# A two-layer encoder in fp32: order of the little products in gate and up, turns between VectorE and GpSimd, and new places

## The chip, the cores and the metric

The kernel runs on one core of a Trainium2 chip. The metric is the device time of one launch in microseconds; lower is better. Three runs of the kernel before took 604.31, 604.35 and 604.79 us, so its median is 604.35 us. TensorE, the matrix engine, is called PE here; DVE is VectorE, ACT is ScalarE, POOL is GpSimd, and SP only issues transfers.

## The reference

Two encoder layers on 256 positions of 1024 features, all in fp32. The mixer projects to three groups of heads (neighbourhood, dilated, grouped-query attention), normalises and rotates, attends, and projects back. The channel sublayer is where most of the time goes:

```python
def channel_sublayer(x, n2, w_gu, cw, cb, w_dn):
    h = rms_norm(x, n2)
    g, u = jnp.split(h @ w_gu, 2, axis=-1)
    g = depthwise_conv_centred(g, cw, cb)
    return x + (jax.nn.gelu(g, approximate=False) * u) @ w_dn

for l in range(DEPTH):                      # DEPTH = 2, S = 256, D_FF = 2816
    x = mixer_sublayer(x, norm1_g[l], w_in[l], q_norm_g[l], k_norm_g[l], rpb[l],
                       out_norm_g[l], w_out[l], tables)
    x = channel_sublayer(x, norm2_g[l], w_gate_up[l], conv_w[l], conv_b[l], w_down[l])
```

## The kernel before

**Products.** An fp32 product is made of three products of split operands: each operand is a rounded high part (hi) and the rest (lo), and hi·hi, hi·lo and lo·hi are summed in PSUM. Weights arrive by DMA as `wp_raw`; for each unit of weights (`unit`, `split`, lines 683 to 715) ScalarE casts raw to `wp_hi` and VectorE subtracts to get `wp_lo`. The layer's input, scaled and transposed by PE and ScalarE, is `act_hT`, whose lo half is made by VectorE (`split_T`, line 731).

**The feed-forward part.** The 2816 features go in 11 steps of two blocks (j = 0, 1) of 128 features. A step has a gate (G), an up (U) and a down (D); the list `FFN` (line 77) gives their order. Gate and up run `half_up` (line 1346) on one unit of weights. For each block there are eight *large* products (a 128x128 piece of the weight's hi against 512 columns, which are hi and lo of the input side by side) and eight *little* ones (a piece of the weight's lo against the 256 columns of the input's hi). All sixteen of a block sum into one PSUM bank, `ps[j]`, a buffer of the pool `psw`. In the rows, large is `psw_w<-act_hT,wp_hi ... 128x512` and little is `psw_w<-act_hT,wp_lo ... 128x256`. The order is large 0, little 0, large 1, little 1, eight each; the first gate of a layer has an order of its own. Down adds 24 matmuls of 512 columns into four banks `psa_a`. In the last step of the last layer the last of its four column pieces is halved, into 256 columns in `psa` and 256 in a bank of `psw` (`end`), so that the output can go out in pieces.

**The order of the work.** Nothing is issued where it is written. Every operation is recorded in a `Plan` (class at line 239), with a cost from `cost` (line 475), and so all instructions show one line in the profile, L472. `Plan.order` (line 323) is a list scheduler: it keeps, for each engine, the time at which it comes free, takes among all ready operations the one that can start first, and among equals the one of the lowest rank. The rank is the operation's number in the program plus a shift for some kinds of work plus an entry of the table `PLACES` (line 229), which moves single operations by hand:

```python
o.rank = i + self.shift + PLACES.get(i, 0)
...
if at is not None and (best is None or (at, o.rank, i) < best):
    best = (at, o.rank, i)
...
else:
    free[e], end = at + o.ns, at + o.lat
```

The order that comes out is fixed at build time. On the chip each engine runs its list in that order, and waits where an operand or a buffer is late.

**The start and the tail.** Before the first projections ScalarE casts the first weights, scales the eight transposes of the input into `act_hT` and squares the input for its norm (`mean_squares`, line 755; `act_s2k<-const_x`). At the end VectorE adds the sums to `const_x` piece by piece (the lines behind `down(last)`, about 1476), and SP sends each piece out.

## Time and profile before

| | |
|---|---|
| median of three runs | 604.35 us |
| the profiled execution's own time | 604.39 us |
| its span in the trace | 602.6 us |
| PE busy | 596.9 us, 3496 matmuls |
| DVE busy | 484.9 us |
| ACT busy | 428.5 us |
| POOL busy | 81.0 us |
| TensorE clock granted | full in every slice |

The busy time of an engine says how much work it has; only the chain that ended last, and the gaps in an engine's timeline, say what bounds the end. A row of a timeline groups neighbouring instructions of one kind: the start of the first, then the time from there to the end of the last, which overlaps the next row since matmuls are pipelined. So the pace of PE is read from start to start.

### The profile page before, as it was taken

Reading aid. Unit: us, or ns where it says so; the run is one execution under the profiler, and the core shown is the slowest. Engines: PE = TensorE matmul, PEld = TensorE weight load, DVE = VectorE, ACT = ScalarE, POOL = GpSimd, SP = SyncE. Lnnn points to the kernel's source line nnn. Section 1 sums busy time; section 2 is a strip of 40 time slices with the busy share of each in tenths; the row PEclk is TensorE's granted clock in tenths of the full one; section 3 lists DMA queues with packets and bytes.
Section 4 is the critical chain, followed back from the end, with each engine's and each line's share of the span. In section 5 each row is a group of like instructions: output and inputs, shape, how many; then the busy total and the mean of one; then the engine's idle time right before and its main releaser. Section 6 shows DMA issues by size and latency. Waiting matters only on the chain.

```text
span 602.6 us, 9916 instructions
## 1 busy us (share of the span) xinstructions
PE 596.9 (99%) x3496; PEld 524.7 (87%) x3496; DVE 484.9 (80%) x995; ACT 428.5 (71%) x1065; POOL 81.0 (13%) x130
## 2 busy tenths in 40 slices
PE   8999999999999999999999999999999999999997
PEld 7999898888888888888899989888888888888886
DVE  4899988997788988888777898777977777777775
ACT  6889999686566767666688899676766556666661
POOL 2733030102400000000023213421000000000000
PEclk9999999999999999999999999999999999999999
DMA  8893313557588898999444726844465556555501
GB/s 281 294 329 114 106 36 108 196 188 238 174 243 292 274 358 310 327 308 298 155 143 159 258 71 245 281 177 140 140 210 202 171 188 210 173 179 208 194 16 70
DMA packets 85218, 121.44 MB, mean 202 GB/s; under 512 B 9881, under 2 KB 69881, under 8 KB 85169
## 3 DMA queue, kind: packets, MB, share of 16 engines
q1 hardware_dynamic: 82896, 112.17, 55.8%
q0 software_dynamic: 1728, 8.39, 4.1%
q8 instruction: 27, 0.44, 0.3%
q10 hardware_dynamic: 544, 0.26, 0.1%
q14 instruction: 23, 0.18, 0.1%
HBM read 110.93 MB, written 9.88 MB: 200 GB/s over the span
## 4 chain that ended last, share of the span: by engine, by line
PE 97%; ACT 1%; DVE 1%; POOL 0%; issue 0%; DVEq 0%; POOLq 0%
PE psw_w L472 53%; PE psa_a L472 44%; ACT act_s2k L472 0%; POOL small_rstd L472 0%; ACT act_z L472 0%; DVE act_z L472 0%; ACT act_hT L472 0%; DVE wp_lo L472 0%; DVE act_sw L472 0%; POOL small_ms L472 0%; DVE const_x L472 0%; DVE act_qo L472 0%; ACT wp_hi L472 0%; POOL const_warm L472 0%; DVEq L472 0%
## 5 line engine op out<-in xcount | busy, mean ns | idle before, releaser
L472 DVE TENSOR_TENSOR wp_lo<-wp_raw,wp_hi 128x512 fp32r<-128x512 f32 (+2 forms) x332 | 231.8, 733 | 57.1 <-ACT wp_hi L472 41.1
L472 ACT CAST wp_hi<-wp_raw 128x512 fp32r<-128x512 f32 (+2 forms) x332 | 203.0, 663 | 21.7 <-PE psw_w L472 10.1
L472 PE MATMUL psw_w<-act_hT,wp_hi 128*128 128x512 f32 x704 | 180.3, 393 | 0.0
L472 PEld LDWEIGHTS psw_w<-act_hT,wp_hi 128*128 128x128 f32 x704 | 127.3, 188 | 24.5 <-DVE act_hT L472 0.6
L472 PE MATMUL psa_a<-wp_hi,act_hT 128*128 128x384 f32 (+2 forms) x448 | 112.6, 331 | 0.7 <-ACT wp_hi L472 0.7
L472 PEld LDWEIGHTS psw_w<-act_hT,wp_lo 128*128 128x128 f32 x704 | 97.2, 188 | 7.1
L472 PE MATMUL psw_w<-act_hT,wp_lo 128*128 128x256 f32 x704 | 101.3, 280 | 0.0
L472 PEld LDWEIGHTS psa_a<-wp_hi,act_hT 128*128 128x128 f32 x448 | 78.2, 188 | 3.4 <-ACT wp_hi L472 0.9
L472 PE MATMUL psa_a<-wp_lo,act_hT 128*128 128x384 f32 (+2 forms) x224 | 74.2, 333 | 0.1
L472 ACT COPY act_s2k<-psw_w 128x256 f32<-128x256 f32 x88 | 32.3, 372 | 58.5 <-PE psw_w L472 58.1
L472 PE MATMUL psa_a<-wp_lo,act_ch 128*128 128x512 f32 (+1 forms) x176 | 68.2, 387 | 0.0
L472 PE MATMUL psa_a<-wp_hi,act_ch 128*128 128x512 f32 x176 | 68.1, 388 | 0.0
L472 PE MATMUL psa_a<-wp_hi,act_cl 128*128 128x512 f32 (+1 forms) x176 | 67.6, 388 | 0.0
L472 DVE TENSOR_TENSOR act_s2k<-psw_w,act_s2k 128x256 f32<-128x256 f32 x88 | 36.7, 422 | 12.2 <-ACT act_s2k L472 11.8
L472 PEld LDWEIGHTS psa_a<-wp_lo,act_hT 128*128 128x128 f32 x224 | 42.1, 188 | 2.3 <-DVE wp_lo L472 1.0
L472 PEld LDWEIGHTS psa_a<-wp_hi,act_cl 128*128 128x128 f32 x176 | 33.1, 188 | 6.8
L472 PEld LDWEIGHTS psa_a<-wp_hi,act_ch 128*128 128x128 f32 x176 | 33.0, 188 | 6.2
L472 PEld LDWEIGHTS psa_a<-wp_lo,act_ch 128*128 128x128 f32 x176 | 33.1, 188 | 6.0
L472 DVE SCALAR_TENSOR_TENSOR act_s2k<-act_s2k,act_cw,act_s2k 128x255 f32<-128x255 f32 x88 | 36.8, 478 | 1.4 <-ACT act_s2k L472 1.3
L472 ACT ACTIVATE act_s2k<-act_s2k 128x512 f32<-128x512 f32 x22 | 13.9, 632 | 30.2 <-DVE act_s2k L472 30.2
L472 ACT ACTIVATE act_s2k<-act_s2k,act_cw 128x256 f32<-128x256 f32 x44 | 24.1, 595 | 15.4 <-DVE act_s2k L472 15.4
L472 POOL TENSOR_TENSOR small_rstd<-small_ms,const_mh 128x6 f32<-128x6 f32 (+2 forms) x26 | 30.8, 1186 | 14.2 <-DVE small_ms L472 12.6
(132 smaller groups left out, 791.7 us busy)
## 6 DMA issues: line engine op xcount, KB each, us to landing
wp_raw<-in_w_gate_up_dram SPq DMA_DIRECT2D x44, 1024.0 KB, 5.0
wp_raw<-in_w_down_dram SPq DMA_DIRECT2D x22, 1024.0 KB, 7.3
wp_raw<-in_w_in_dram SPq DMA_DIRECT2D x14, 768.0 KB, 5.9
wp_raw<-in_w_in_dram SPq DMA_DIRECT2D x8, 1024.0 KB, 7.0
wp_raw<-in_w_out_dram SPq DMA_DIRECT2D x8, 768.0 KB, 7.8
dram_khi<-act_mixT_hi SPq DMA_DIRECT2D x4, 768.0 KB, 3.6
dram_klo<-act_mixT_lo SPq DMA_DIRECT2D x4, 768.0 KB, 8.4
wp_lo<-dram_klo POOLq DMA_DIRECT2D x4, 768.0 KB, 5.0
```

What stands on the lines that cost most here:

```text
L472: getattr(o.engine.real, o.method)(*map(real, o.args), **{k: real(v) for k, v in o.kw.items()})
```

## The change

Four edits. `half_up` takes the second block's little products ahead of its large ones, so that sixteen little ones follow each other. The scheduler's model gives VectorE and GpSimd turns: while one of them runs an operation that `port` names, an operation of that kind on the other is planned to start later. Some cost constants are new. And the table `PLACES` is new, with some 170 entries in place of some 50.

```diff
 PLACES = {
-    375: -35, 488: 15, 528: -53, 550: 173, 587: -78, 594: 125, 616: -286, 646: -9, 709: -79, 750: -226, 752: -396,
...
+    51: 278, 85: 457, 93: -352, 125: 200, 153: 280, 169: 468, 171: 497, 174: 74, 188: -31, 189: -346, 190: -296,
...
@@ Plan.add
+        o.port = port(engine.name, method, kw, ins)
@@ Plan.order
+        held = {"DVE": 0.0, "POOL": 0.0}
...
-                free[e], end = at + o.ns, at + o.lat
+                wait = 0.0
+                if o.port == "both":
+                    wait = max(0.0, held["POOL"] - at)
+                    held["DVE"] = at + wait + o.ns
+                elif o.port:
+                    wait = max(0.0, held["DVE"] - at - 100)
+                    held["POOL"] = at + wait + (o.ns if o.port == "long" else 160)
+                free[e], end = at + wait + o.ns, at + wait + o.lat
@@ cost
-        ns = {512: 231.6, 384: 174.5, 256: 118.0}.get(n, n / 2.25 + 2.5)
+        ns = {512: 228.0, 384: 173.8, 256: 117.8}.get(n, n / 2.25 + 2.5)
...
     elif method == "tensor_copy":
-        ns = 0.92 * n + 100
+        ns = 0.98 * n + 100
     elif kw.get("op") == ALU.pow:
-        ns = 560 + 150 * n
+        ns = 380 + 157 * n
     elif method == "tensor_scalar":
-        ns = 350 + 3.8 * n
+        ns = 270 + 1.7 * n
     else:
-        ns = 830 if out.width() == S else 350 + 3.1 * n
+        ns = 180 + 2.19 * n
     return ns, ns - 95, 0, None
+
+
+def port(engine, method, kw, ins):
+
+    inside = [v for v in ins if not v.tile.pool.psum]
+    if engine == "DVE" and method in ("tensor_tensor", "scalar_tensor_tensor"):
+        wide = [v for v in inside if v.width() > 1]
+        return "both" if len(wide) == 2 and len(inside) == len(ins) else None
+    if engine == "POOL" and method in ("tensor_tensor", "tensor_scalar", "tensor_copy"):
+        return "short" if kw.get("op") == ALU.pow else "long"
+    return None
@@ half_up
-            def large(j, k):
-                nc.tensor.matmul(ps[j], wh[:, k, j * P : (j + 1) * P], h2[:, k], start=k == 0, stop=False)
+            def large(j, k, start, stop):
...
+            def little(j, k, start, stop):
...
-            for j in range(2):
-                for k in range(KD):
-                    large(j, k)
-                for k in range(KD):
-                    little(j, k)
+            for j, kinds in enumerate(((large, little), (little, large))):
+                for part_ in kinds:
+                    for k in range(KD):
+                        part_(j, k, part_ is kinds[0] and k == 0, part_ is kinds[1] and k == KD - 1)
```

The three places below are shown as the engine's list stands before and after. The new kernel's records have line L490.

PE, one step's gate and up in the first layer's feed-forward part; `psw_w...` are the banks, `wp_hi`/`wp_lo` the split weights. Before:

```order
L472 MATMUL psw_w1_117<-act_hT0_146,wp_hi1_240 128x512 x8
L472 MATMUL psw_w1_117<-act_hT0_146,wp_lo1_248 128x256 x8
L472 MATMUL psw_w3_166<-act_hT0_146,wp_hi1_240 128x512 x8
L472 MATMUL psw_w3_166<-act_hT0_146,wp_lo1_248 128x256 x8
L472 MATMUL psw_w0_83<-act_hT0_146,wp_hi0_141 128x512 x8
L472 MATMUL psw_w0_83<-act_hT0_146,wp_lo0_149 128x256 x8
L472 MATMUL psw_w2_124<-act_hT0_146,wp_hi0_141 128x512 x8
L472 MATMUL psw_w2_124<-act_hT0_146,wp_lo0_149 128x256 x8
```

Now:

```order
L490 MATMUL psw_w1_117<-act_hT0_146,wp_hi1_230 128x512 x8
L490 MATMUL psw_w1_117<-act_hT0_146,wp_lo0_149 128x256 x8
L490 MATMUL psw_w0_83<-act_hT0_146,wp_lo0_149 128x256 x8
L490 MATMUL psw_w0_83<-act_hT0_146,wp_hi1_230 128x512 x8
L490 MATMUL psw_w3_163<-act_hT0_146,wp_hi0_141 128x512 x8
L490 MATMUL psw_w3_163<-act_hT0_146,wp_lo1_236 128x256 x8
L490 MATMUL psw_w2_124<-act_hT0_146,wp_lo1_236 128x256 x8
L490 MATMUL psw_w2_124<-act_hT0_146,wp_hi0_141 128x512 x8
```

The runs of eight little products have become runs of sixteen, with two blocks of large ones next to each other between them; in the whole program 113 runs of little products have become 83, of which 32 are of exactly sixteen.

ACT, the end of its work on the first input: scaled transposes (`act_hT`), squares (`act_s2k<-const_x`) and the casts of weight unit 1 (`wp_raw1`). Before:

```order
L472 ACTIVATE act_hT0_146<-psw_w1_117,const_gains0_122 128x256 x2
L472 ACTIVATE act_s2k4_223,small_ssx0_163<-const_x0_79 128x512
L472 ACTIVATE act_hT0_146<-psw_w2_124,const_gains0_122 128x256 x2
L472 ACTIVATE act_s2k0_81,small_ssx0_163<-const_x0_79 128x512
L472 CAST wp_hi1_240<-wp_raw1_138 128x384 x4
L472 CAST wp_hi0_141<-wp_raw2_153 128x384 x4
```

Now:

```order
L490 ACTIVATE act_hT0_146<-psw_w1_117,const_gains0_122 128x256 x2
L490 ACTIVATE act_s2k4_221,small_ssx0_165<-const_x0_79 128x512
L490 CAST wp_hi1_230<-wp_raw1_138 128x384
L490 ACTIVATE act_hT0_146<-psw_w2_124,const_gains0_122 128x256
L490 CAST wp_hi1_230<-wp_raw1_138 128x384 x3
L490 ACTIVATE act_s2k0_81,small_ssx0_165<-const_x0_79 128x512
L490 ACTIVATE act_hT0_146<-psw_w2_124,const_gains0_122 128x256
L490 CAST wp_hi0_141<-wp_raw2_153 128x384 x4
```

The casts of unit 1 have moved ahead of the last square and of the last two scaled transposes.

DVE, its last additions into `const_x`, each behind the last matmul of its bank. Before:

```order
L472 SCALAR_TENSOR_TENSOR const_x0_79<-psa_a2_302,small_rx1_1587,const_x0_79 128x512
L472 SCALAR_TENSOR_TENSOR const_x0_79<-psa_a3_332,small_rx1_1587,const_x0_79 128x512
L472 SCALAR_TENSOR_TENSOR const_x0_79<-psa_a1_175,small_rx1_1587,const_x0_79 128x512
L472 SCALAR_TENSOR_TENSOR const_x0_79<-psw_w0_83,small_rx1_1587,const_x0_79 128x256
L472 SCALAR_TENSOR_TENSOR const_x0_79<-psa_a0_157,small_rx1_1587,const_x0_79 128x512
```

Now:

```order
L490 SCALAR_TENSOR_TENSOR const_x0_79<-psa_a1_179,small_rx1_1581,const_x0_79 128x512
L490 SCALAR_TENSOR_TENSOR const_x0_79<-psa_a0_156,small_rx1_1581,const_x0_79 128x512
L490 SCALAR_TENSOR_TENSOR const_x0_79<-psa_a2_291,small_rx1_1581,const_x0_79 128x512
L490 SCALAR_TENSOR_TENSOR const_x0_79<-psa_a3_321,small_rx1_1581,const_x0_79 128x512
L490 SCALAR_TENSOR_TENSOR const_x0_79<-psw_w3_163,small_rx1_1581,const_x0_79 128x256
```

The piece that goes out last is now 256 columns wide instead of 512.

## Rows read from the trace of the kernel before

**Rows 1.** The page: busy time of each engine, and the chain that ended last by engine.

```profile
PE 596.9 (99%) x3496; PEld 524.7 (87%) x3496; DVE 484.9 (80%) x995; ACT 428.5 (71%) x1065; POOL 81.0 (13%) x130
...
PE 97%; ACT 1%; DVE 1%; POOL 0%; issue 0%; DVEq 0%; POOLq 0%
```

**Rows 2.** Timeline of PE, end of the first unit: start us, us, engine, operation, count.

```profile
13.21 0.28 PE L472 MATMUL psw_w<-const_warm 128*128 128x256 bf16 x1
14.16 0.62 PE L472 MATMUL psa_a<-wp_hi,act_hT 128*128 128x384 f32 x2 [0.67 <-ACT wp_hi L472]
```

**Rows 3.** Timeline of PE around 34.4 us.

```profile
34.25 0.33 PE L472 MATMUL psa_a<-wp_lo,act_hT 128*128 128x384 f32 x1
34.42 0.34 PE L472 MATMUL psa_a<-wp_hi,act_hT 128*128 128x384 f32 x1
34.84 0.44 PE L472 MATMUL psa_a<-wp_lo,act_hT 128*128 128x384 f32 x1
```

**Rows 4.** The chain that ended last, in order of time: one step's gate and up.

```profile
160.16 11.12 PE psw_w L472 x64
```

**Rows 5.** Timeline of PE, the same step's first two blocks.

```profile
160.00 1.98 PE L472 MATMUL psw_w<-act_hT,wp_hi 128*128 128x512 f32 x8
161.81 1.10 PE L472 MATMUL psw_w<-act_hT,wp_lo 128*128 128x256 f32 x8
162.75 2.02 PE L472 MATMUL psw_w<-act_hT,wp_hi 128*128 128x512 f32 x8
164.60 1.11 PE L472 MATMUL psw_w<-act_hT,wp_lo 128*128 128x256 f32 x8
165.55 1.99 PE L472 MATMUL psw_w<-act_hT,wp_hi 128*128 128x512 f32 x8
```

**Rows 6.** Timeline of PE, runs of four, six and ten little products.

```profile
178.38 0.64 PE L472 MATMUL psw_w<-act_hT,wp_lo 128*128 128x256 f32 x4
178.85 2.03 PE L472 MATMUL psw_w<-act_hT,wp_hi 128*128 128x512 f32 x8
180.72 1.11 PE L472 MATMUL psw_w<-act_hT,wp_lo 128*128 128x256 f32 x8
...
289.06 0.87 PE L472 MATMUL psw_w<-act_hT,wp_lo 128*128 128x256 f32 x6
289.76 1.99 PE L472 MATMUL psw_w<-act_hT,wp_hi 128*128 128x512 f32 x8
291.59 1.34 PE L472 MATMUL psw_w<-act_hT,wp_lo 128*128 128x256 f32 x10
292.76 0.40 PE L472 MATMUL psa_a<-wp_hi,act_ch 128*128 128x512 f32 x1
...
294.63 0.40 PE L472 MATMUL psa_a<-wp_hi,act_cl 128*128 128x512 f32 x1
```

**Rows 7.** Timeline of ACT before the casts of unit 1.

```profile
12.98 0.64 ACT L472 ACTIVATE act_s2k<-const_x 128x512 f32<-128x512 f32 x1
...
13.59 0.93 ACT L472 CAST wp_hi<-wp_raw 128x384 fp32r<-128x384 f32 x2
```

**Rows 8.** Timeline of DVE, its last two additions.

```profile
596.88 0.48 DVE L472 SCALAR_TENSOR_TENSOR const_x<-psw_w,small_rx,const_x 128x256 f32<-128x256 f32 x1
598.70 0.75 DVE L472 SCALAR_TENSOR_TENSOR const_x<-psa_a,small_rx,const_x 128x512 f32<-128x512 f32 x1 [1.34 <-PE psa_a L472]
```

**Rows 9.** Transfers, 594 to 603: GB/s in 40 slices; issues, KB each, us to landing.

```profile
GB/s 0 0 0 0 0 0 0 0 0 200 419 355 191 300 373 382 310 337 82 350 196 0 0 0 0 0 0 0 346 400 364 55 0 0 0 0 0 0 0 0
...
out_dram<-const_x SPq DMA_DIRECT2D x3, 256.0 KB, 2.0
```

**Rows 10.** Timeline of POOL and DVE, 24 to 27 us.

```profile
24.11 2.16 POOL L472 COPY act_nab<-small_few 28x1984 f32<-28x1984 f32 x1
...
24.49 1.96 DVE L472 TENSOR_TENSOR act_sw<-act_z,small_sdq 128x48 f32<-128x48 f32 x2
```

**Rows 11.** Windows: us, busy us (count) of PE, PEld, DVE, ACT, POOL, clock, DMA share, GB/s.

```profile
15.00:30.00 15.00, 15.00 (x90) 14.97 (x90) 12.38 (x27) 12.46 (x68) 11.25 (x17) 1.00 0.87 295
30.00:45.00 15.00, 14.92 (x88) 14.57 (x87) 14.42 (x31) 12.13 (x41) 5.71 (x14) 1.00 1.09 328
```

More of the change, by code (lines that the diff above doesn't have):

```diff
@@ L206 @@
 class Op:
-    __slots__ = ("engine", "method", "args", "kw", "ns", "lat", "kind", "size", "tiles", "first", "before", "after", "left", "at", "rank", "burst")
+    __slots__ = ("engine", "method", "args", "kw", "ns", "lat", "kind", "size", "tiles", "first", "before", "after", "left", "at", "rank", "burst", "port")
 class PlanEngine:
@@ L1349, in half_up @@
             ps = [psw.tile([P, 2, S], F32, tag="w", name=f"{name}{j}") for j in range(2)]
-            def large(j, k):
-                nc.tensor.matmul(ps[j], wh[:, k, j * P : (j + 1) * P], h2[:, k], start=k == 0, stop=False)
-            def little(j, k):
+            def large(j, k, start, stop):
                 nc.tensor.matmul(
-                    ps[j][:, 0], wl[:, k, j * P : (j + 1) * P], h2_hi[:, k], start=False, stop=k == KD - 1
+                    ps[j], wh[:, k, j * P : (j + 1) * P], h2[:, k], start=start, stop=stop, skip_group_check=True
+                )
+            def little(j, k, start, stop):
+                nc.tensor.matmul(
+                    ps[j][:, 0], wl[:, k, j * P : (j + 1) * P], h2_hi[:, k], start=start, stop=stop,
+                    skip_group_check=True,
                 )
             def part(j, k):
-                large(j, k)
-                little(j, k)
+                large(j, k, k == 0, False)
+                little(j, k, False, k == KD - 1)
             if first:
@@ L1375, in half_up @@
                 return ps
-            for j in range(2):
-                for k in range(KD):
-                    large(j, k)
-                for k in range(KD):
-                    little(j, k)
+            for j, kinds in enumerate(((large, little), (little, large))):
+                for part_ in kinds:
+                    for k in range(KD):
+                        part_(j, k, part_ is kinds[0] and k == 0, part_ is kinds[1] and k == KD - 1)
             return ps
```

19 rows, old and new, of the table PLACES are left out of this document.

## The prediction

> **What bounds the kernel now.** The page's busy shares come first: TensorE (PE) is busy for 596.9 of 602.6 us with 3496 matmuls, and the chain that ended last runs through it for 97% of the span [rows 1]. So a change is worth what it does to PE's own time, to the few places where PE waits, and to what lies before its first and behind its last matmul. The profiled execution took 604.39 us against its span of 602.6, so 1.8 us lie around the span; I sum against 604.39, which is 0.04 us over the median of 604.35. A measurement of this kernel can tell about 0.2% (1.2 us) from no change, so "faster" means below 603.14 and "slower" above 605.56.
>
> Next, PE's timeline, for gaps. There is one of 0.67 us at 14.16, put down to a cast of a weight on ScalarE [rows 2], and a short one around 34.4 us, where a matmul that could follow 0.17 us behind its forerunner, as the one before did, starts 34.84 - 34.42 = 0.42 us behind it [rows 3]: a wait of about 0.25 us. I found no other that comes near these. In the feed-forward part, where most of the time lies, matmul follows matmul: the 64 of one step's gate and up take 11.12 us on the chain [rows 4], and there are 11 such steps in each of two layers.
>
> Inside the step the order matters a little [rows 5]. Eight large products (512 columns) that follow a down take 161.81 - 160.00 = 1.81 us; behind a run of eight little ones (256 columns) they take 164.60 - 162.75 = 1.85. Eight little ones take 162.75 - 161.81 = 0.94 or 165.55 - 164.60 = 0.95 us by the starts around them. So the border from 256 to 512 columns costs some 0.04 us, and one has to ask what it costs behind sixteen.
>
> **The change part by part.**
>
> *The order in gate and up.* No matmul is added or taken away. A regular step had four runs of eight little ones; it now has two of sixteen, with two blocks of large ones in a row between them. Of sixteen no row exists. What the trace has is runs of other lengths [rows 6]: behind a run of four, eight large ones take 180.72 - 178.85 = 1.87 us; behind six, 291.59 - 289.76 = 1.83; behind ten (eight matmuls of down, of the same width) 294.63 - 292.76 = 1.87. Read as a pattern with period three, 4 and 10 are alike and dear, 6 is cheap, and 16 falls with 4 and 10. That is three lengths and my reading of them, not a proof. I take 1.87 because ten is the nearest length, and 1.82 for a block of larges directly behind such a block (0.01 above the plain 1.81, an estimate for an offset that has to settle). The four blocks of a step then take 1.81 + 1.87 + 1.82 + 1.87 = 7.37 us, against 11.12 - 4 x 0.94 = 7.36 before: +0.01. If a run of sixteen is left like one of six, they take 1.81 + 1.83 + 1.81 + 1.83 = 7.28, or -0.08. The new order has 32 runs of exactly sixteen, which is 16 steps' worth: +0.2 or -1.3. The other six steps' worth, which the scheduler cuts up, keeps as many borders as it had (113 runs of little ones in the whole program before, 83 after, 30 fewer, where the regular steps alone have 32 fewer), with runs of other lengths; as a dear border and a cheap one differ by up to 0.06 us, I put that at -0.1, between -0.4 and +0.2. The feed-forward term is **+0.1 us**, bounds -1.7 and +0.4.
>
> The Trainium skill's page "TensorE: Matmul & The Clock Gate", section "Wait — 56ns, not 53.3ns?", lets warm matmuls start N / 2.4 GHz + about 2.5 ns apart, with no term for what went before; by it the order is worth 0.0 us whatever the run length. The trace does not agree to the hundredth: 1.81, 1.85 and 1.87 us for eight matmuls of one width.
>
> The edit brings no new wait. Block 0's little products needed all eight lo pieces already, and they come straight behind its large ones as before; block 1's little ones use the same lo pieces. Bank 0 is still finished after 16 matmuls and bank 1 after 32, so ScalarE's copies and VectorE's sums behind them can start as before.
>
> *The start.* Before, ScalarE makes eight scaled transposes and four squares, and only then the casts of weight unit 1; the first comes at 13.59, behind a square that began at 12.98 [rows 7]. PE has its last work before that at 13.21 (a filler) and goes on at 14.16 [rows 2]. The new order puts the first cast of unit 1 ahead of one square and two scaled transposes: at least the 13.59 - 12.98 = 0.61 us of the square earlier on ScalarE. PE can gain at most 14.16 - 13.21 = 0.95. Between these ends I take **-0.8 us**, as two scaled transposes go the same way as the square; the bounds are -0.95 and 0 (a gain that is lost before the end).
>
> *The tail.* Before, the last group is 512 wide, VectorE's addition behind it takes 0.75 us from 598.70 [rows 8], and then 256 KB go out, which takes 2.0 us to landing [rows 9]. After, the last group is the 256-wide one. The same addition at 256 columns took 0.48 us at 596.88 [rows 8], so -0.27. The transfer is half as large: the last four slices of 0.225 us in which the output's queue moves anything, at 346, 400, 364 and 55 GB/s, are the 256 KB [rows 9], some 0.8 us, so half of them saves about 0.4; if the transfer's time is fixed, it saves nothing. Together **-0.65 us**, bounds -0.27 and -0.7.
>
> *VectorE and GpSimd take turns.* The trace shows what the scheduler now models: beside GpSimd's copy of 2.16 us at 24.11, two VectorE multiplications of 48 columns took 1.96 us together [rows 10]. The model only reorders, and as PE waited for VectorE nowhere but at 34.4, taking turns can give PE at most 0.25 us. The new costs of a matmul (228.0 for 231.6 ns at 512 columns) and of GpSimd change nothing but order too. The table of places moves instructions all over the attention part. What hides them is PE's stock of ready work: PE is busy for 14.92 of 15 us even from 30 to 45, where VectorE is busy for 14.42 [rows 11]. If a cast comes later than that stock lasts, the loss is that lateness in full. I take **0**, nearest to the rows without a gap, bounds -0.25 and +2.16 (the longest single hold shown).
>
> Sum: 604.39 - 0.8 - 0.65 + 0.1 + 0 = 603.04, less 0.04 to the median: **603.0 us**.
>
> **The rivals.**
>
> *The start's gain is eaten on the way.* If ScalarE and VectorE keep their own pace up to 34.4, PE arrives early and waits longer, as the 0.25 us there show it can [rows 3]. For it: VectorE's 14.42 of 15 us from 30 to 45. Against it: from 15 to 30 it is busy for 12.38 only and can work ahead [rows 11]. Time: 604.35 - 0.65 + 0.1 = 603.8 us, no measurable change.
>
> *Sixteen is a cheap run.* My period of three rests on three lengths. Then the feed-forward term is -1.3 - 0.1 = -1.4 in place of +0.1, and the time 603.0 - 1.5 = 601.5, or down to 600.9 where the other open terms come out at their low ends too (-0.15 at the start, -0.05 at the tail, -0.25 at 34.4).
>
> *GpSimd's copy holds VectorE, and VectorE holds PE (slower).* The copy act_nab of 2.16 us stands behind other work on GpSimd now. If it falls on a stretch in which VectorE makes the lo piece that PE needs next, VectorE stands for up to 2.16 us, the other pieces queue behind it on VectorE, and PE waits. It decides from the point where PE's slack against the lo pieces, nothing at 34.4, is under the hold. Such a wait swallows the start's gain: 604.35 - 0.65 + 0.1 + 2.16 = 606.0 us. For it: VectorE is nearly full from 30 to 45. Against it: the new scheduler knows of the hold, and the hold at 24.5 cost PE nothing before.
>
> *The change does not do what it says.* The model of taking turns may be wrong for the chip; as it works on order alone, that ends in one of the times above.
>
> **How the numbers follow.** The forecast as summed has a chance of 0.46, the eaten start 0.28, the cheap sixteen 0.14, the held VectorE 0.12. The forecast lies 0.1 us below the bound of "faster", and its open terms reach further down than up, so about 0.32 of its 0.46 counts as faster and 0.14 as the same; with the cheap case, and 0.01 for a start that is eaten in part, faster has 0.47. Of the held case 0.09 is over 605.56 and the rest, a smaller hold, is the same: 0.44 for the same. The range reaches down to the cheap case's end, 600.9, and up to 604.9, an eaten start with half a hold (603.8 + 1.1); beyond it I leave about 0.1 above and 0.05 below.
>
> **What would show it.** Right: PE goes on with unit 1 near 13.4 instead of 14.16 and has no new wait up to 35; eight large ones behind sixteen little ones in 1.87 us and 64 matmuls of gate and up in 11.1 us; a last VectorE addition of about 0.48 us, and an end of the span some 3.3 us behind that addition's start instead of 602.6 - 598.70 = 3.9. Wrong: a wait of PE over 0.5 us for a hi or lo piece between 15 and 130 us; 1.83 us behind sixteen, and 11.04 for the 64; a PE busy time that differs from 596.9 by more than 1.5 us; a new wait in the feed-forward part for a bank or a lo piece.

## Result and profile after

The changed kernel took **605.92 us** (median of 12 runs, 604.98 to 607.28) beside 604.43 us (12 runs) for the kernel before on the same chip: a ratio of **1.0027, interval 1.0020 to 1.0035**. It is slower: 605.92 lies above the 605.56 that the prediction set as its bound, and the interval begins at 0.2%. The forecast was 603.0 with a range of 600.9 to 604.9. The profiled execution took 606.49 us with a span of 604.7 (before: 604.39 and 602.6).

The page's busy times of the engines, and the chain that ended last [rows 1]:

```profile
PE 598.3 (99%) x3496; PEld 523.6 (87%) x3496; DVE 484.9 (80%) x995; ACT 427.1 (71%) x1065; POOL 83.5 (14%) x130
...
PE 70%; DVE 11%; ACT 6%; POOL 4%; DMA 4%; issue 3%; SPq 1%; POOLq 0%
```

No engine has much more work. But the chain ran through PE for 97% before, and for 70% now: it leaves PE for VectorE, ScalarE, GpSimd and the transfers. The 30% outside PE are not time that PE lost, as PE is busy for 99% in both; they say that the work of other engines now decides when PE's work can start.

**Where the time went.** Both traces hold all 3496 matmuls, so the n-th can be compared in time at the borders of the stages:

| start of | before | after | the stage alone |
|---|---|---|---|
| 61st product of 384 columns (start) | 20.76 | 19.68 | -1.08 |
| 780th matmul, gate and up of layer 0 begin | 119.78 | 120.76 | +2.06 |
| 1709th, gate and up of layer 0 end | 292.65 | 293.88 | +0.25 |
| 2507th, gate and up of layer 1 begin | 414.85 | 417.33 | +1.25 |
| last matmul | 598.27 | 600.93 | +0.18 |
| end of the span | 602.60 | 604.72 | -0.54 |

The start gave its gain, and so did the tail. The stages between lost 2.06 + 0.25 + 1.25 + 0.18 = 3.74 us, most of it in the attention parts of the two layers. (The 61st product marks the same products, not the same amount of other work, so the first two rows are sure in their sum, +0.98, rather than one by one. They are also one execution each. With the order of before up to there, the 780th matmul began between 119.25 and 120.37 in seven traces (before, e1, t1, b1, c1, e5, h1, of which b1 has one cast exchanged); with that of after, at 120.76, 120.15 and 120.23 (after, e2, h2).)

**The start.** ScalarE's casts of unit 1 and PE's products behind them, on the timeline [rows 2, 7]:

```profile
12.02 0.51 ACT L490 CAST wp_hi<-wp_raw 128x384 fp32r<-128x384 f32 x1
...
12.79 1.34 ACT L490 CAST wp_hi<-wp_raw 128x384 fp32r<-128x384 f32 x3
...
12.86 0.68 PE L490 MATMUL psa_a<-wp_hi,act_hT 128*128 128x384 f32 x3
```

The first cast begins at 12.02 instead of 13.59, and the wait of 0.67 us at 14.16 is gone.

**Sixteen little products** and the large ones behind them, PE's timeline [rows 5, 6]:

```profile
201.95 2.05 PE L490 MATMUL psw_w<-act_hT,wp_lo 128*128 128x256 f32 x16
203.84 2.02 PE L490 MATMUL psw_w<-act_hT,wp_hi 128*128 128x512 f32 x8
205.70 0.39 PE L490 MATMUL psa_a<-wp_hi,act_ch 128*128 128x512 f32 x1
```

From start to start the eight large ones take 205.70 - 203.84 = 1.86 us here. Behind 30 of the 32 runs of sixteen they take 1.87, behind one 1.82.

**The tail.** VectorE's last addition and the output's transfers [rows 8, 9]:

```profile
601.25 0.48 DVE L490 SCALAR_TENSOR_TENSOR const_x<-psw_w,small_rx,const_x 128x256 f32<-128x256 f32 x1 [0.69 <-PE psw_w L490]
```
```profile
out_dram<-const_x SPq DMA_DIRECT2D x3, 256.0 KB, 2.0
out_dram<-const_x SPq DMA_DIRECT2D x2, 128.0 KB, 1.9
```

The addition takes 0.48 instead of 0.75. The transfer of half the size lands after 1.9 us instead of 2.0.

**New waits of PE.** The view of PE's waits by what ended them: total us, times, longest. (Left out is the 1.0 us before the first input, which the kernel before has too.)

```profile
PE psw_w L490 <- ACT act_s2k L490: 0.9, 2, 0.8
PE psa_a L490 <- DMA wp_hi<-dram_khi: 0.3, 1, 0.3
PE psw_w L490 <- DVE wp_lo L490: 0.3, 1, 0.3
```

The largest, near 50 us, is followed back through three engines on the timeline:

```profile
44.31 2.08 DVE L490 SCALAR_TENSOR_TENSOR act_nab<-act_nab,const_na 128x576 f32<-128x576 f32 x3
...
45.38 1.16 POOL L490 TENSOR_SCALAR small_ms<-small_ss,small_he 128x6 f32<-128x6 f32 x1 [8.96 <-ACT act_s2k L490]
...
46.62 1.32 POOL L490 TENSOR_TENSOR small_rstd<-small_ms,const_mh 128x6 f32<-128x6 f32 x1
...
47.97 0.56 DVE L490 TENSOR_TENSOR act_z<-psa_a,small_rstd 128x384 f32<-128x384 f32 x1 [1.24 <-POOL small_rstd L490]
...
48.04 0.28 POOL L490 TENSOR_SCALAR small_ms<-small_ss,small_he 128x6 f32<-128x6 f32 x1
...
49.53 0.28 PE L490 MATMUL psa_a<-wp_lo,act_hT 128*128 128x256 f32 x1
...
50.00 0.91 ACT L490 ACTIVATE act_s2k<-act_s2k,small_rs 128x256 f32<-128x256 f32 x2
...
50.56 0.33 PE L490 MATMUL psw_w<-const_ident,act_s2k 128*128 128x128 f32 x1 [0.75 <-ACT act_s2k L490]
```

GpSimd's `small_ms` takes 1.16 us while VectorE runs the three additions, and 0.28 at 48.04 when they are over. VectorE then waits 1.24 us for `small_rstd`; scaling, softmax and ScalarE's `act_s2k` are late behind it; and PE, which has run out of other work, starts 50.56 - 49.53 = 1.03 us after its last matmul, where 256 columns take 0.12: 0.91 us lost.

The wait at 31.4 has GpSimd's copy behind it, with `small_rstd` late for ScalarE's scaling and the cast behind that:

```profile
24.98 2.15 POOL L490 COPY act_nab<-small_few 28x1984 f32<-28x1984 f32 x1
...
29.83 1.13 ACT L490 ACTIVATE act_z<-psa_a,small_rstd 128x64 f32<-128x64 f32 x5 [0.96 <-POOL small_rstd L490]
...
30.84 0.53 ACT L490 CAST wp_hi<-wp_raw 128x384 fp32r<-128x384 f32 x1
```

In the feed-forward part of layer 0, where the copy for layer 1 is made, GpSimd holds VectorE directly:

```profile
143.60 3.80 DVE L490 TENSOR_TENSOR wp_lo<-wp_raw,wp_hi 128x512 fp32r<-128x512 f32 x3 [1.13 <-PE psa_a L490]
144.06 1.93 POOL L490 COPY act_nab<-small_few 28x1984 f32<-28x1984 f32 x1 [19.48 <-DMA small_few<-in_rpb_dram]
...
150.63 0.97 PE L490 MATMUL psw_w<-act_hT,wp_lo 128*128 128x256 f32 x6 [0.29 <-DVE wp_lo L490]
```

Of the three `wp_lo` the middle one took 2.33 us instead of 0.69. VectorE then works without a gap up to the `wp_lo` that ends PE's wait: PE starts at 150.63, 0.45 us later than usual, and its next step takes 0.11 more.

Read as steps from start to start less the usual ones, PE's waits come to 0.40 us at 31.4, 0.91 at 50.6, 0.12 at 120.8 (0.28, where before had 0.16), 0.56 at 150.6, 0.34 at 360.6 (a matmul that waits 0.18 us for ScalarE), 0.37 at 378.4 and 0.62 at 399.0 (a `wp_hi` that is loaded behind its `wp_lo`): together 3.3 us, of which 2.6 in the attention parts. Read in the same way, the wait at 34.8 that the kernel before had and after has not was 0.35 us. So 3.0 of the 3.74 us are accounted for; the other 0.8 is spread over steps too small to name, and was not located.

### The profile page after: what moved, and what is told of

It is laid out like the page before. It is cut to its first block, busy times and chain, and to the rows that moved or that the text cites. A ratio compares the mean times of both kernels' runs of the same rounds, so it can differ in the third digit from the quotient of the medians.

```text
span 604.7 us, 9886 instructions
## 1 busy us (share of the span) xinstructions
PE 598.3 (99%) x3496; PEld 523.6 (87%) x3496; DVE 484.9 (80%) x995; ACT 427.1 (71%) x1065; POOL 83.5 (14%) x130
## 4 chain that ended last, share of the span: by engine, by line
PE 70%; DVE 11%; ACT 6%; POOL 4%; DMA 4%; issue 3%; SPq 1%; POOLq 0%
PE psw_w L490 42%; PE psa_a L490 28%; ACT act_s2k L490 4%; DVE wp_lo L490 3%; POOL small_rstd L490 2%; DMA wp_hi<-dram_khi 2%; DMA const_gk<-in_k_norm_g_dram 1%; DVE act_cl L490 1%; DVE act_z L490 1%; DVE act_s2k L490 1%; ACT wp_hi L490 1%; DMA const_x<-in_x_dram 1%; DVE const_x L490 1%; ACT act_ch L490 1%; POOL small_ms L490 1%
## 5 line engine op out<-in xcount | busy, mean ns | idle before, releaser
L490 DVE TENSOR_TENSOR wp_lo<-wp_raw,wp_hi 128x512 fp32r<-128x512 f32 (+2 forms) x332 | 234.9, 738 | 51.4 <-ACT wp_hi L490 46.9
L490 ACT CAST wp_hi<-wp_raw 128x512 fp32r<-128x512 f32 (+2 forms) x332 | 204.3, 665 | 37.0 <-PE psw_w L490 21.0
L490 PE MATMUL psw_w<-act_hT,wp_hi 128*128 128x512 f32 x704 | 177.3, 393 | 0.1
L490 PEld LDWEIGHTS psw_w<-act_hT,wp_hi 128*128 128x128 f32 x704 | 128.6, 188 | 25.8 <-DVE act_hT L490 0.5
L490 PE MATMUL psa_a<-wp_hi,act_hT 128*128 128x384 f32 (+2 forms) x448 | 114.7, 333 | 0.1
L490 PEld LDWEIGHTS psw_w<-act_hT,wp_lo 128*128 128x128 f32 x704 | 92.7, 188 | 5.1 <-DVE wp_lo L490 0.7
L490 PE MATMUL psw_w<-act_hT,wp_lo 128*128 128x256 f32 x704 | 96.5, 280 | 0.3 <-DVE wp_lo L490 0.3
L490 PEld LDWEIGHTS psa_a<-wp_hi,act_hT 128*128 128x128 f32 x448 | 78.1, 188 | 3.0 <-ACT wp_hi L490 0.5
L490 PE MATMUL psa_a<-wp_lo,act_hT 128*128 128x384 f32 (+2 forms) x224 | 74.1, 332 | 0.0
L490 PE MATMUL psa_a<-wp_lo,act_ch 128*128 128x512 f32 (+1 forms) x176 | 68.3, 388 | 0.0
L490 PE MATMUL psa_a<-wp_hi,act_ch 128*128 128x512 f32 (+1 forms) x176 | 67.8, 388 | 0.0
L490 ACT COPY act_s2k<-psw_w 128x256 f32<-128x256 f32 x88 | 32.1, 371 | 50.3 <-PE psw_w L490 50.3
L490 PE MATMUL psa_a<-wp_hi,act_cl 128*128 128x512 f32 (+1 forms) x176 | 64.2, 387 | 0.0
L490 DVE TENSOR_TENSOR act_s2k<-psw_w,act_s2k 128x256 f32<-128x256 f32 x88 | 36.4, 420 | 23.1 <-ACT act_s2k L490 23.1
L490 PEld LDWEIGHTS psa_a<-wp_lo,act_hT 128*128 128x128 f32 x224 | 42.1, 188 | 2.1 <-DVE wp_lo L490 0.8
L490 PEld LDWEIGHTS psa_a<-wp_hi,act_ch 128*128 128x128 f32 x176 | 33.1, 188 | 6.9
L490 PEld LDWEIGHTS psa_a<-wp_hi,act_cl 128*128 128x128 f32 x176 | 33.1, 188 | 6.7 <-DVE act_cl L490 0.2
L490 PEld LDWEIGHTS psa_a<-wp_lo,act_ch 128*128 128x128 f32 x176 | 33.1, 188 | 6.6
L490 DVE SCALAR_TENSOR_TENSOR act_s2k<-act_s2k,act_cw,act_s2k 128x255 f32<-128x255 f32 x88 | 37.3, 481 | 0.8 <-ACT act_s2k L490 0.7
L490 POOL TENSOR_TENSOR small_rstd<-small_ms,const_mh 128x6 f32<-128x6 f32 (+2 forms) x26 | 32.1, 1236 | 16.9 <-DVE small_ms L490 15.3
L490 ACT ACTIVATE act_s2k<-act_s2k,act_cw 128x256 f32<-128x256 f32 x44 | 24.1, 596 | 12.7 <-DVE act_s2k L490 12.6
L490 ACT ACTIVATE act_s2k<-act_s2k,small_rs 128x256 f32<-128x256 f32 x64 | 29.5, 516 | 0.4 <-DVE small_rs L490 0.3
```

Source lines behind the costliest of these rows:

```text
L490: getattr(o.engine.real, o.method)(*map(real, o.args), **{k: real(v) for k, v in o.kw.items()})
```

## Experiments

Each ratio is against the kernel before on the same chip, five rounds.

**One edit at a time.** *e1*: before, with the order of gate and up alone.

```diff
-            for j in range(2):
-                for k in range(KD): large(j, k)
-                for k in range(KD): little(j, k)
+            for j, kinds in enumerate(((large, little), (little, large))):
+                for part_ in kinds:
+                    for k in range(KD): part_(j, k, ...)
```

> The kernel before with the new order in gate and up alone (old costs, no turns, old places), so the mixer of layer 0 is issued exactly as before. Theory A (the time went into the mixer parts, where PE of the changed kernel waits 0.9 us at 49.5 and in smaller pieces): the new order is worth +0.1 to +0.3 us, so 604.4 to 604.8, ratio 0.9995 to 1.0010; eight large ones behind sixteen little ones take 1.87 us. Theory B (the new order makes PE wait for lo pieces in the feed-forward part, as at 150.0 of the changed kernel): 605.2 to 606, ratio 1.0015 or more, and new gaps of 0.3 us or more in the feed-forward part.

Measured: 606.04 us, **1.0029 (1.0020 to 1.0038)**: the time of theory B, but not by its wait, as PE waits for a `wp_hi` and not for a `wp_lo`. The first attention part keeps its order; the loss begins in the feed-forward part (stage of gate and up of layer 0: +1.05 us). PE's and ScalarE's timeline there:

```profile
187.17 0.62 PE L472 MATMUL psw_w<-act_hT,wp_lo 128*128 128x256 f32 x4
187.62 0.63 PE L472 MATMUL psw_w<-act_hT,wp_hi 128*128 128x512 f32 x2
...
187.82 0.37 ACT L472 COPY act_s2k<-psw_w 128x256 f32<-128x256 f32 x1 [1.39 <-PE psw_w L472]
188.09 0.62 ACT L472 CAST wp_hi<-wp_raw 128x512 fp32r<-128x512 f32 x1
...
188.77 2.56 PE L472 MATMUL psw_w<-act_hT,wp_hi 128*128 128x512 f32 x8 [0.51 <-ACT wp_hi L472]
```

With the large products last, the `wp_hi` buffer is in use to the end of gate or up, while before the block's eight little products (0.94 us) gave ScalarE time to cast the next weights into it. ScalarE's view of waits says the same: total us, times, longest, before, then e1, then after:

```profile
ACT wp_hi L472 <- PE psw_w L472: 10.1, 17, 1.1
```
```profile
ACT wp_hi L472 <- PE psw_w L472: 26.1, 18, 2.3
```
```profile
ACT wp_hi L490 <- PE psw_w L490: 21.0, 16, 1.5
```

In after PE waits for no `wp_hi` there; what in its order covers the longer hold was not looked at. In e1 PE loses 1.3 us between 187.9 and 191.2.

*e2*: after, with the old order of gate and up.

```diff
-            for j, kinds in enumerate(((large, little), (little, large))):
+            for j, kinds in enumerate(((large, little), (large, little))):
```

> The changed kernel with the old order in gate and up (turns, costs and places new). Theory A: 605.4 to 606.2, ratio 1.002 to 1.003, with the wait of 0.9 us at 49.5 still there. Theory B: back to 604.0 to 604.8.

Measured: 608.03 us, 1.0054 (1.0041 to 1.0067), over the range of either theory and 2.1 us over after (1.6 by the ratios). The wait near 50 us is there, so it does not come from the order of gate and up; new ones stand between 147 and 156. The table of places was made for the new order.

*e3*: before with the turns and the new costs, old table, old order. *e4*: after with the old table, so e3 with the new order. Against after:

```diff
 PLACES = {
-    51: 278, 85: 457, 93: -352, ...
+    375: -35, 488: 15, 528: -53, ...
```

> The kernel before with turns and new costs, with the old places and the old order in gate and up. Theory A in its first form (the new table of places does the harm): 604.0 to 604.9, ratio within 0.001 of 1. In its second form (planning in turns with the new costs moves the mixer's work so that PE waits, whatever the table): 605.3 or more. Theory B: as before, 604.4.

> The changed kernel with the old places: turns, new costs and the new order in gate and up. Theory A: as the run with turns and costs alone, within 0.3 us. Theory B: 0.8 us or more above that run.

Measured: e3 612.17 us, **1.0130 (1.0116 to 1.0144)**, theory A in its second form; e4 614.4, **1.0158 (1.0144 to 1.0173)**, theory B. PE's waits in e3:

```profile
PE psw_w L481 <- POOL small_rx L481: 1.7, 1, 1.7
...
PE psw_w L481 <- DVE act_hT L481: 1.4, 1, 1.4
...
PE psa_a L481 <- DMA wp_hi<-dram_khi: 0.9, 1, 0.9
```

The new costs are nearer to the rows (280 ns for GpSimd's `small_ms`, which takes 0.28 us, where the old ones gave 373), but with a table made for the old ones they cost 7.9 us. The new table takes 614.4 - 605.9 = 8.5 us off again. (It has 150 entries, not some 170; the old one has 56.) And the new order costs about 2 us in both places where the table was not made for it (e1 +1.8; e4 over e3 +2.2, or 1.7 by the ratios, with a mean granted clock of 0.997 in three of e4's five executions), and saves 2.1, or 1.6 by the ratios, where it was (e2 against after).

**Halves of the program.** *h1* takes start and attention of both layers from before and the rest from after; *h2* is the reverse. Each engine's order is written out as a list, joined from the two.

```diff
 h1: start, attention 0 | gate, up, down 0 | attention 1 | gate, up, down 1, tail
-    after              | after            | after       | after
+    before             | after            | before      | after
```

> The changed kernel's new order in gate and up, its feed-forward parts and its tail, with both mixers (and the start) issued as in the kernel before; the order of every engine is read from a list that joins the two planned orders. Theory A (the mixers' new order costs some 2 us, the feed-forward parts about 0.4, the tail gives back 0.45): 604.0 to 604.9, ratio 0.9995 to 1.001, and no wait of PE over 0.3 us up to 119 us. Theory B (the feed-forward parts hold the loss, by lo and hi pieces that come late): 605.3 to 606.2.

> The reverse: old order in gate and up and the feed-forward parts and tail of the kernel before, with the start and both mixers issued as in the changed kernel. Theory A: 605.8 to 607.0, ratio 1.0025 or more, with the wait of 0.9 us near 50.5. Theory B: 603.5 to 604.6 (the start's gain of 1 us is kept and nothing is lost).

Measured: h1 605.75 us, 1.0021 (1.0012 to 1.0030); h2 608.0, 1.0060 (1.0048 to 1.0072). By the times alone h1 is in theory B's range and h2 over theory A's. But joined lists make waits of their own. In h1 four waits between 304.9 and 418 add up to 1.3 us (0.37, 0.25, 0.35 and 0.35); in h2 one at 419.3 alone is

```profile
419.33 0.33 PE L562 MATMUL psw_w<-const_ident,const_x 128*128 128x128 f32 x1 [1.56 <-DVE const_x L562]
```

on PE's timeline. The wait near 50 us stays in h2 with 0.96 us, so it belongs to the new attention order. How the loss divides between the halves the two runs do not tell.

**The wait near 50 us.** *m1*: after, with the three additions of 576 columns moved a little back on VectorE.

```diff
-DVE  act_nab<-act_nab,const_na  128x576  x3
 DVE  act_z<-psa_a,small_rstd  128x384
+DVE  act_nab<-act_nab,const_na  128x576  x3
```

> The changed kernel with three VectorE instructions moved: the additions into act_nab (128x576, three in a row at 44.3) now stand behind the scaling of act_z that waits for GpSimd at 47.97. Theory A2 (these three hold GpSimd's small_ms, which took 1.16 us at 45.38 where its like takes 0.28, and through it PE's transposes at 50.56): small_ms takes 0.3 us, the wait of 0.9 us near 50.5 falls under 0.2, and the time falls by 0.6 to 1.0 us to 604.9 to 605.3. Rival (the transposes wait for ScalarE's own queue, or PE waits for something else a little later): the wait stays or comes back within 10 us, and the time stays at 605.6 to 606.2.

Measured: 607.25 us, **1.0046 (1.0034 to 1.0058)**, slower still. The timeline of GpSimd, VectorE and PE:

```profile
45.39 0.27 POOL L566 TENSOR_SCALAR small_ms<-small_ss,small_he 128x6 f32<-128x6 f32 x1 [8.95 <-ACT act_s2k L566]
...
47.58 2.10 DVE L566 SCALAR_TENSOR_TENSOR act_nab<-act_nab,const_na 128x576 f32<-128x576 f32 x3
...
51.71 0.33 PE L566 MATMUL psw_w<-const_ident,act_s2k 128*128 128x128 f32 x1 [1.88 <-ACT act_s2k L566]
```

The hold is shown: without the additions beside it `small_ms` takes 0.27 us for 1.16. But the additions now stand ahead of the softmax on VectorE, and their 2.10 us are worth more than the 0.89 gained. On an engine that works in order a delay is not cured by moving it a little.

*m2*: the same three moved far back, into stretches before 61.5, 77.5 and 79.1 us.

```diff
-DVE  act_nab<-act_nab,const_na  128x576  x3     (at 44.3)
+DVE  act_nab<-act_nab,const_na  128x576         (ahead of 61.5, 77.5, 79.1; one each)
```

> The changed kernel with the same three additions into act_nab moved much further back on VectorE, one each to a place where it stood idle (before 61.5, 77.5 and 79.1 us); nothing else is moved. Theory A2: GpSimd's small_ms takes 0.3 us as in the run before, and now nothing new stands ahead of the softmax of the transposes, so that PE's wait of 0.9 us near 50.5 falls under 0.2 and the time by 0.7 to 1.0, to 604.9 to 605.2, ratio 1.0008 to 1.0015. Rival: PE's gain is taken back by a later wait, as ScalarE is full from 45 to 60: no wait near 50.5, others up to 119 us that add up to 0.5 or more, and 605.6 to 606.

Measured: 605.16 us, **1.0011 (1.0002 to 1.0019)**, as expected.

```profile
44.93 0.28 POOL L566 TENSOR_SCALAR small_ms<-small_ss,small_he 128x6 f32<-128x6 f32 x1 [8.91 <-ACT act_s2k L566]
...
49.24 0.33 PE L566 MATMUL psw_w<-const_ident,act_s2k 128*128 128x128 f32 x1
...
61.79 0.44 PE L566 MATMUL psw_w<-const_ident,act_s2k 128*128 128x128 f32 x2 [0.51 <-DVE act_cl L566]
```

PE no longer waits at 49.24, where it had at 50.56. A new, smaller wait stands at 61.79, where the first addition went. *m3* and *m4* mend three more waits of after; m4 also puts the first addition some 16 us later again (the three before 77.5, 79.1 and 80.9).

```diff
 DVE  three act_nab additions: m3 as m2, m4 one each ahead of 77.5, 79.1, 80.9
+ACT  one cast wp_hi  ahead of  five act_z scalings   (wait at 31.4)
+DVE  act_cl          ahead of  an act_z scaling      (wait at 378.4)
+POOL load of wp_hi   ahead of  the load of wp_lo     (wait at 399.0)
```

> The run before with three more moves, each at a new wait of PE: ScalarE's cast of a weight ahead of five scalings that stand for GpSimd (31.4 us, 0.3), VectorE's act_cl ahead of a scaling that stands for GpSimd (378.4, 0.26), and the load of a kept weight's hi half ahead of its lo half (399.0, 0.5). Theory A (the loss is the sum of such waits): together with their start-up gaps of 0.1 each 1.4 us below the run before, 603.5 to 603.9, ratio 0.998 to 0.9995. Rival (one wait hides the next): 604.5 to 605.2.

> The run with four repaired waits, but with none of the three moved additions ahead of the scaling at 61.5, where VectorE was late for PE by 0.65 us in it: they stand before 77.5, 79.1 and 80.9 us now. Theory A (the changed kernel's loss is the sum of PE's new waits): that wait goes too, -0.5 to -0.7 against that run, 604.0 to 604.4, ratio 0.998 to 1.0005. Rival: a later place pays (PE waits between 77 and 100 us), ratio as before, 1.001.

Measured: m3 604.89 us, 1.0010 (0.9998 to 1.0022), a miss: the wait of m2 near 61 stays with 0.65 us, and the one behind GpSimd's copy at 144 with 0.45. m4: 604.45 us, **0.9999 (0.9990 to 1.0009)**. Six instructions put elsewhere give back the whole loss of after against before. They do not bring the forecast: 604.45 is still 1.45 us over it. From the 61st product to the 780th matmul its trace takes 99.9 us and that of m3 100.3, for 99.0 in before, and where that goes was not located. (The execution of m4 that was profiled took 605.76, so it is no guide to the median; on its PE timeline one repaired wait is turned over, now for the `wp_lo` that is loaded second:)

```profile
398.51 0.51 PE L566 MATMUL psa_a<-wp_lo,act_mixT_hi 128*128 128x512 f32 x1 [0.79 <-DMA wp_lo<-dram_klo]
```

**Start and tail alone.** *t1*: before, with the tail of after. *st*: with its start (to 21 us) too. *b1*: t1, and the first cast of unit 1 ahead of the last square and nothing else.

```diff
 t1, PE and DVE: the 256-wide sum comes last instead of last but one;
     one cast of wp_hi and its wp_lo move with it
 st, as t1, and every engine's order up to 21 us as in after
 b1, as t1, and on ACT:
+    CAST wp_hi1<-wp_raw1 128x384
     ACTIVATE act_s2k<-const_x 128x512
-    CAST wp_hi1<-wp_raw1 128x384
```

> The kernel before with the changed kernel's tail alone (the order behind the last up, with the group of 256 columns last). By the trace of the changed kernel, where the span ends 3.8 us behind the start of the last matmul instead of 4.3: -0.55 us, 603.8 to 604.0, ratio 0.9985 to 0.9995. Rival: the transfers of the last pieces stand in line and the end stays: 604.4.

> The kernel before with two pieces of the changed kernel's order: the start up to 21 us and the tail behind the last up. Theory A (the start gains 1.0 us, the tail 0.45, both reach the end): 602.7 to 603.4, ratio 0.997 to 0.9985. Rival (the start's gain is eaten on the way, at the wait near 34.4 or by ScalarE and VectorE, which keep their pace): 603.8 to 604.1, ratio 0.999 to 0.9995, with a wait of PE of 0.5 us or more between 21 and 60 us.

> The kernel before with the changed kernel's tail, and of its start one exchange alone: the first cast of weight unit 1 ahead of the last square on ScalarE, so that GpSimd's statistics come 0.4 us later and not 1.7 as in the changed start. PE goes on with unit 1 near 13.6 instead of 14.2; if nothing eats it, -0.5 beside the tail's -0.5: 603.2 to 603.5, ratio 0.998 to 0.9988. Rival (any later statistics hold VectorE and PE, as in the run with the whole start): a wait of 0.4 us or more between 20 and 35 us, and the tail's ratio alone, 0.9988 to 0.9995.

Measured: t1 603.79 us, **0.9992 (0.9983 to 1.0000)**; st 604.6, **1.0003 (0.9993 to 1.0014)**; b1 603.87, **0.9990 (0.9982 to 0.9999)**. In all three the span ends 3.8 us behind the start of the last matmul, where it was 4.33 in before; so the tail is worth the 0.5 us that was expected of t1, though the interval of t1's ratio reaches 1.0000. The start is worth nothing beside it: the 61st product comes at 19.88 in st, for 20.92 in t1, but the 780th matmul at 120.56, for 119.80. On the timeline of st:

```profile
25.16 1.83 POOL L551 COPY act_nab<-small_few 28x1984 f32<-28x1984 f32 x1
25.24 0.56 DVE L551 TENSOR_TENSOR act_z<-psa_a,small_rstd 128x384 f32<-128x384 f32 x1 [1.22 <-POOL small_rstd L551]
...
25.71 1.40 DVE L551 TENSOR_TENSOR act_z<-act_z,act_sw 128x96 f32<-128x96 f32 x1
...
27.63 0.44 PE L551 MATMUL psa_a<-wp_lo,act_hT 128*128 128x384 f32 x1 [0.97 <-DVE wp_lo L551]
```

The squares, moved back for the casts, feed GpSimd's `small_rstd`, which comes 1.7 us later; VectorE waits 1.22 us for it and is then held by the copy (1.40 us for 96 columns), and the `wp_lo` behind it are late: PE gives back 1.14 and 0.31 us. In b1 one cast alone changes places with the square, and PE meets the `wp_lo` instead of the `wp_hi`:

```profile
14.87 0.44 PE L551 MATMUL psa_a<-wp_lo,act_hT 128*128 128x384 f32 x1 [0.46 <-DVE wp_lo L551]
```

**How the order of gate and up costs.** *e5*: before, with the little products on the outside, so that the `wp_hi` is free early. *c1*: e1, with the old order in the one half-step before the wait at 188, and two casts moved ahead of a copy there.

```diff
 e5:
-            for j, kinds in enumerate(((large, little), (little, large))):
+            for j, kinds in enumerate(((little, large), (large, little))):
 c1:
+            second = (large, little) if name == "G0_4" else (little, large)
-            for j, kinds in enumerate(((large, little), (little, large))):
+            for j, kinds in enumerate(((large, little), second)):
```

> The kernel before with another order in gate and up alone: little 0, large 0, large 1, little 1, so that the large products lie in a run of sixteen and the hi half is again out of use eight little products before the end. Theory C (the new order alone costs 1.7 us because it holds the hi half to the end of the unit, and ScalarE's next cast into that buffer has no cover): no wait of PE for a cast of hi near 188 us, 604.2 to 604.8, ratio under 1.001, unless the lo half, which is now wanted 1.8 us sooner, comes late (then PE waits for VectorE's wp_lo, which the profile names). Rival (the loss of the new order alone is the borders between widths or a changed plan as such): a ratio of 1.002 or more without such waits.

> The kernel with the new order in gate and up alone, whose order of all engines is kept from its plan, but in one half-step (gate of step 4 in layer 0, before PE's wait of 0.7 us near 188) the old order is back, so that its hi half is out of use eight little products earlier, and ScalarE's first two casts into that buffer stand ahead of a copy. Theory C (the held hi half is what the new order alone pays for at that place): no wait of PE for a cast near 188, the pieces of 1.3 us between 187.9 and 191.2 go, and the time falls by 0.9 to 1.3 us against the run with the new order alone, to a ratio of 1.0005 to 1.0015. Rival (the plan around it is late anyway): a wait of 0.5 us or more stays within 5 us of that place.

Measured: e5 609.69 us, 1.0093 (1.0078 to 1.0108); c1 606.53, 1.0030 (1.0018 to 1.0042). e5 does what it should for the buffer (between 150 and 290 us ScalarE's casts wait 3.0 us for PE's gate and up, against 11.4 in e1), and PE waits for no `wp_hi` there. But its plan comes out otherwise, and PE waits for something else, after which its clock falls. PE's timeline, and the windows behind it (stretch, length, busy time of PE, PEld, DVE, ACT and POOL with the instructions of each, granted clock, share of the DMA engines, GB/s):

```profile
190.66 0.50 PE L472 MATMUL psa_a<-wp_hi,act_ch 128*128 128x512 f32 x1 [3.09 <-ACT act_ch L472]
```
```profile
190.60:192.10 1.50, 1.44 (x6) 1.24 (x7) 1.50 (x5) 1.00 (x3) 0.00 (x0) 1.00 0.81 232
192.10:195.60 3.50, 3.50 (x10) 2.71 (x9) 2.65 (x6) 1.25 (x2) 0.00 (x0) 0.51 1.03 403
```

So e5's total says nothing of the hold itself. In c1 the step at 188.8 is 0.24 us too long instead of 0.68, but

```profile
191.06 0.50 PE L552 MATMUL psa_a<-wp_hi,act_ch 128*128 128x512 f32 x1 [1.01 <-ACT act_ch L552]
```

PE waits some 2 us later for `act_ch`: the rival, that the plan around is late. That the held buffer makes the wait at 188 agrees with the view of ScalarE's waits and with c1; but c1 moves a copy as well, and the two were not tried apart. That the hold is the whole cost of the new order in e1 is not shown, and how those 1.8 us divide stays open.

## Why the prediction was wrong

- **"VectorE and GpSimd take turns … I take 0"**: this is the step that failed. The order that turns, costs and places make together has PE wait 3.3 us in all, against 0.35 that it took away at 34.8; the bound was +2.16. Moving six instructions takes 1.5 us back (605.92 to 604.45, m4), and the three additions alone 0.8 (m2). I read the cover from PE's share (14.92 of 15 us), but that says only that PE did not wait, not by how much: VectorE's 14.42 of 15 us, in the same row [rows 11], told of little slack. The chain that ended last, of which I took only the share of 97%, said it outright. In the kernel before it leaves PE at 25.1 us and comes back at 34.84, by way of GpSimd's statistics (start us, us):

```profile
26.56 0.90 POOL small_ms L472
27.53 1.52 POOL small_rstd L472
...
34.26 0.54 DVE wp_lo L472
```

  On that path PE had no lead. After's third `small_rstd` ends at 29.80 instead of 29.05, and PE, which now comes earlier, waits at 31.4.
- **The rival "GpSimd's copy holds VectorE"** named the mechanism, at a chance of 0.12; that its time comes out (606.0 us, for 605.92) is luck. It added one hold of 2.16 us to a start that gains nothing, where the trace has waits of 3.3 us in seven places and a start that gains 1.08. The place was another, too: the largest loss runs from VectorE's additions to GpSimd, and only those of 0.40 and 0.56 us at 31.4 and 150.6 have the copy behind them.
- **"The new scheduler knows of the hold"** was taken as evidence against that rival. By the code, `port` is asked with the inputs that `Plan.add` has kept, and `Plan.add` drops an input that is the output's own view; so the additions `act_nab<-act_nab,const_na` count as one wide input, and no turn is planned for them. Nor can an order fix when the copy at 144.06 starts, since its transfer sets that. (In the kernel before it fell at 146.41, where VectorE soon had nothing to do.) This is read from the code and the timelines and was not tried.
- **"The edit brings no new wait"** holds for banks and `wp_lo`, which I named, and fails for the third buffer, `wp_hi`: e1, in which the edit stands alone, loses 1.8 us. In after PE waits for no `wp_hi` in that part, but ScalarE's casts wait 21.0 us for PE in place of 10.1.
- **Sixteen little products**: 1.87 measured, 1.87 taken, so the price of the border was right and the cheap rival (1.83) fell; the period of three behind it was not tested. The stages of gate and up moved by +0.25 and +0.18 us, with 0.56 us of waits in the first of them.
- **The start**: PE had its 1.08 us by 19.68 (0.8 taken; it passed the bound of 0.95, which left out that in before the three steps behind the wait took 0.28 to 0.31 us each instead of 0.17), and lost it by 50.56. "The start's gain is eaten on the way" held, and st shows it without any other edit: tail and start together are worth nothing measurable.
- **The tail**: -0.54 of the -0.65 taken. From the start of the last matmul to that of the addition it is 0.32 us instead of 0.43, as the matmul is shorter too; the addition gave its 0.27; and behind it 2.99 us are left instead of 3.15. So the transfer's 0.4 was too much: its landing takes 1.9 us for 2.0.
- **The signs**: PE went on at 12.86 us, and its busy time differs by 1.4 us, as it should have been. The sign of a wait over 0.5 us for a hi or lo piece before 130 us did not show although the forecast was wrong: the 0.91 us were for `act_s2k`, which I had not thought of. The one of a wait for a lo piece in the feed-forward part did, at 150.6.
- **The range**: its low end does not follow from its terms. 601.5 - 0.15 - 0.05 - 0.25 is 601.05, not 600.9.
- The sum, then: -1.08 + 2.06 + 0.25 + 1.25 + 0.18 - 0.54 = +2.1 us in the profiled executions, +1.5 between the medians; forecast -1.4.

The fastest version tried is before with the tail alone (t1) or with one cast moved as well (b1), 0.8 to 1.0 parts in a thousand under before and less than the 1.2 us that can be told for sure.

## What to carry to other kernels

On a list-scheduled kernel whose bounding engine never waits, ask of each edit which buffer it holds longer and how much sooner than needed each operand was ready; a gap view shows only where that lead is already gone, and the chain that ended last shows the stretches where it leaves that engine. A table of hand-made places fits one plan: the new table was worth 8.5 us with the model it was made for, and that model with the old table cost 7.9. And work brought forward on an engine that runs in order pushes something back, so follow what was pushed as far as what was brought.

## What the runs showed of the hardware

- The hold between VectorE and GpSimd goes both ways: `small_ms` on GpSimd took 1.16 us for 0.28 beside VectorE's additions, and `wp_lo` on VectorE 2.33 for 0.69 beside GpSimd's copy. `small_ms` came at 45.38, in the second of three additions without a gap between them, and ended at 46.54, behind the third (46.39).
- In e5 PE's granted clock was still 1.00 for 1.5 us after the wait of 3.09 us, and then 0.51, the level of 1.2 GHz, for 3.5 us, in which a product of 512 columns took 427 ns for 227: some 1.6 us on top of the wait. In e4 the same followed a wait of 2.06 us: PE began again at 404.95, and from 406.0 to 407.5 its granted clock was 0.50.
- After a wait PE's first step is about 0.1 us longer than usual (at 378.45 and 398.97 in after: 0.22 us for 0.12, 0.34 for 0.23).
- With the same order up to there, the 780th matmul began at 119.78 us in before and at 120.37 in e1. The first weights landed later in e1: ScalarE's first cast, which waited for them, began at 6.91 us instead of 5.33.
